# A dilated attention layer laid out by token parity, with values as the stationary operand

## The chip, the cores and the metric

The kernel runs on one core of a Trainium2 chip. The metric is the device time of one execution in microseconds; lower is better. Three runs of the kernel before took 1760.48, 1762.76 and 1765.39 us, so its time is given as the median, 1762.76.

## What is computed

Four transformer layers on 256 tokens of 1024 features, each a mixer and a SwiGLU block with residuals, then one hybrid layer. The mixers are differential attention (layers 0 and 3), latent attention (layer 1) and dilated attention (layer 2); the change is in the last. Its core in the reference:

```
qkv = (h @ w_qkv).reshape(B, S, G, 3, C_HEADS, C_HEAD_DIM)   # G = 3 groups, 16 heads of 64
for g, (window, dilation) in enumerate(((128, 1), (512, 4), (2048, 16))):
    o_g, l_g = _dilated_group(q[:, :, g], k[:, :, g], v[:, :, g], window, dilation)
wts = softmax(stack(lses), axis=0)
o = sum(wts[..., None] * stack(outs), axis=0)
return o.reshape(B, S, C_HEADS * C_HEAD_DIM) @ w_o
```

Here h is the normed input. With 256 tokens, group 0 lets a token attend to tokens at most 64 away; group 1 to all tokens of the same remainder by 4; group 2 to all of the same remainder by 16. Each group has its own softmax and log-sum (`l_g`), and the three outputs are mixed by a softmax over those. All of it is float32.

## The kernel before, in words

Every projection runs in three matmuls per block, since operands are split into a high and a low part of a reduced float32 (`mm3`, lines 184 to 191: high by high, high by low, low by high). `wload` (line 152) fetches a unit of weights (1024 elements in each of 128 partitions), ACT makes its high part (line 158) and DVE its low part (line 159); four raw and six split units can be held. One unit feeds twelve matmuls of 512 columns, six for each of the two tiles of 128 tokens.

The normed input is kept transposed (`hT`, features on partitions, tokens in the columns) and split. `Prep` makes it: `turn` transposes a block of x on PE, DVE multiplies by the gain (L318), ACT writes the high part (L283) and DVE the low part (L284). The factor of each token's norm, `r`, is applied later, where a projection's result is taken out of PSUM. `Prep.half` is called four times, by token tile and half of the features, as the last block of the layer before is added to x.

`layer_c` is the dilated layer. It works group by group in the order (0, first eight heads), (2, both halves), (1, both halves), (0, last eight heads). For groups 1 and 2 the tokens are first put in an order in which those that attend to each other lie side by side: `permuted` copies hT, high part on ACT (L696) and low part on DVE (L698), and the norms go over DRAM by POOL's queue. Within a `step`: queries and keys are projected; their rotation is four DVE operations that end at L384; they are transposed on PE (`to_T`, drained from the list `waiting`); scores come from `qkT` (L735), two heads at a time on the two halves of the rows, 192 keys wide in group 0 and 128 in the others; `heads` adds the mask and takes the maximum on DVE (L537) and the exponential on ACT (L542); `tr4` transposes four blocks of probabilities on PE (L291) into a PSUM bank, which ACT (L524) or DVE (L526) copies out; the values are projected; and the product (L263, by `Chain`, which keeps its matmuls in order) has a 128 x 128 block of probabilities as its stationary operand and 64 columns of values moving. Its output has tokens on partitions. For groups 1 and 2 it goes through DRAM back to the order of tokens, and so do the maxima and sums (`spread`). `dilated` and `total` work out the weights (`merge`) and sum the groups (`wsum`, L860 to L862); the result `on` is transposed on PE and split into `oT` for the output projection (`outacc`), whose first half is issued after both halves of the heads.

PSUM has eight banks: four under the tag acc, two under E, two under T. Tiles of 512 to 1024 elements come from pools of a fixed number of buffers (nine `big` ones of 2048 elements).

The order of the work is set when the program is built: for each engine the framework takes, of the instructions that its own model has as ready, the one that stands earliest in the program, and the engine then runs them in that order. `pump` and `drain` say where in the program the postponed transposes stand. The latent layer (`layer_b`) has a product of another form, which the prediction uses: there the values are stationary and the probabilities move, and heads alternate between the halves of the output partitions.

## Time and profile before

| | us |
|---|---|
| three runs | 1760.48, 1762.76 (median), 1765.39 |
| the profiled execution | 1763.19 |
| its span, first to last instruction | 1761.3 |
| PE busy | 1728.4 |
| DVE busy | 1094.5 |
| ACT busy | 920.0 |
| POOL busy | 75.0 |

The engines are PE (matmuls and transposes; its weight loads are shown as PEld), DVE (element-wise work), ACT (functions and copies), POOL (small work and some transfers) and SP (transfers). A busy time is the union of an engine's instructions. Matmuls overlap each other in the pipeline, so the durations of single ones (some 0.4 us) are longer than the steps between their starts (some 0.23 us); what a matmul costs is read from the steps. Idle time of an engine other than the bounding one costs nothing by itself.

### The profile page before, as it was taken

Reading aid. Unit: us, or ns where it says so; the run is one execution under the profiler, and the core shown is the slowest. Engines: PE = TensorE matmul, PEld = TensorE weight load, DVE = VectorE, ACT = ScalarE, POOL = GpSimd, SP = SyncE. Lnnn points to the kernel's source line nnn. Section 1 sums busy time; section 2 is a strip of 40 time slices with the busy share of each in tenths; the row PEclk is TensorE's granted clock in tenths of the full one; section 3 lists DMA queues with packets and bytes.
Section 4 is the critical chain, followed back from the end, with each engine's and each line's share of the span. In section 5 each row is a group of like instructions: output and inputs, shape, how many; then the busy total and the mean of one; then the engine's idle time right before and its main releaser. Section 6 shows DMA issues by size and latency. Waiting matters only on the chain.

```text
span 1761.3 us, 24095 instructions
## 1 busy us (share of the span) xinstructions
PE 1728.4 (98%) x8944; PEld 1411.0 (80%) x8944; DVE 1094.5 (62%) x1955; ACT 920.0 (52%) x1489; POOL 75.0 (4%) x100
## 2 busy tenths in 40 slices
PE   8999999999999999999999999999999999899998
PEld 6688888877888878788878888877888888688886
DVE  6766545786555575555686744677877567574544
ACT  6655444675444465655655444565544454664443
POOL 1000000101000010000100000000000000010000
PEclk9999999999999999999999999999999999899999
DMA  7346666433666564555545666543567678456662
GB/s 259 112 128 180 185 187 184 148 121 95 187 194 185 177 160 125 163 161 165 159 118 170 187 184 190 176 136 131 167 216 234 190 249 223 144 155 194 190 186 89
DMA packets 168764, 299.53 MB, mean 170 GB/s; under 512 B 20120, under 2 KB 36464, under 8 KB 167880
## 3 DMA queue, kind: packets, MB, share of 16 engines
q1 hardware_dynamic: 164936, 293.52, 54.9%
q0 software_dynamic: 3712, 4.49, 1.0%
q8 instruction: 70, 1.15, 0.3%
q14 instruction: 46, 0.38, 0.1%
HBM read 288.20 MB, written 8.68 MB: 169 GB/s over the span
## 4 chain that ended last, share of the span: by engine, by line
PE 86%; issue 5%; DVE 4%; ACT 2%; DMA 2%; POOL 1%; SPq 0%; POOLq 0%; DVEq 0%; ACTq 0%
PE psacc L191 13%; PE psacc L190 12%; PE psacc L189 12%; PE psE L189 6%; PE psE L191 6%; PE psE L190 6%; PE psT L189 6%; PE psT L190 6%; PE psT L191 6%; PE psT L291 4%; PE psT L263 3%; PE psE L735 2%; PE psE L442 2%; DVE lo L159 1%; PE psE L291 1%
## 5 line engine op out<-in xcount | busy, mean ns | idle before, releaser
L159 DVE TENSOR_TENSOR lo<-raw,hi 128x1024 fp32r<-128x1024 f32 (+1 forms) x528 | 637.3, 1211 | 474.7 <-ACT hi L158 473.2
L158 ACT ACTIVATE hi<-raw 128x1024 fp32r<-128x1024 f32 (+1 forms) x528 | 552.9, 1048 | 588.3 <-PE psacc L191 248.9
L189 PE MATMUL psacc<-hi,big 128*128 128x512 f32 (+1 forms) x1136 | 455.3, 401 | 0.2 <-ACT big L283 0.2
L191 PE MATMUL psacc<-hi,big 128*128 128x512 f32 (+1 forms) x1136 | 449.1, 395 | 0.0
L190 PE MATMUL psacc<-lo,big 128*128 128x512 f32 (+1 forms) x1136 | 447.9, 394 | 0.0
L191 PEld LDWEIGHTS psacc<-hi,big 128*128 128x128 f32 x1136 | 213.8, 188 | 44.9 <-issue 4.2
L190 PEld LDWEIGHTS psacc<-lo,big 128*128 128x128 f32 x1136 | 214.1, 188 | 43.4 <-issue 3.9
L189 PEld LDWEIGHTS psacc<-hi,big 128*128 128x128 f32 x1136 | 214.2, 189 | 40.5 <-issue 1.3
L189 PE MATMUL psE<-hi,big 128*128 128x512 f32 (+2 forms) x568 | 215.3, 379 | 1.0 <-ACT big L283 0.9
L191 PE MATMUL psE<-hi,big 128*128 128x512 f32 (+2 forms) x568 | 213.6, 376 | 0.2 <-DVE big L284 0.2
L190 PE MATMUL psE<-lo,big 128*128 128x512 f32 (+2 forms) x568 | 213.7, 376 | 0.0
L189 PE MATMUL psT<-hi,big 128*128 128x512 f32 (+1 forms) x480 | 178.4, 372 | 0.0
L191 PE MATMUL psT<-hi,big 128*128 128x512 f32 (+1 forms) x480 | 178.3, 372 | 0.0
L190 PE MATMUL psT<-lo,big 128*128 128x512 f32 (+1 forms) x480 | 178.3, 371 | 0.0
L189 PEld LDWEIGHTS psE<-hi,big 128*128 128x128 f32 x568 | 107.6, 189 | 21.0 <-ACT big L283 2.0
L191 PEld LDWEIGHTS psE<-hi,big 128*128 128x128 f32 x568 | 107.5, 189 | 19.0 <-DVE big L284 0.6
L190 PEld LDWEIGHTS psE<-lo,big 128*128 128x128 f32 x568 | 107.5, 189 | 18.4 <-issue 0.4
L189 PEld LDWEIGHTS psT<-hi,big 128*128 128x128 f32 x480 | 90.4, 188 | 15.8 <-issue 0.2
L191 PEld LDWEIGHTS psT<-hi,big 128*128 128x128 f32 x480 | 90.4, 188 | 15.7
L190 PEld LDWEIGHTS psT<-lo,big 128*128 128x128 f32 x480 | 90.4, 188 | 15.6
L542 ACT ACTIVATE p<-psE,st 128x256 f32<-128x256 f32 x96 | 44.5, 472 | 23.5 <-DVE st L540 21.6
L542 ACT ACTIVATE p<-sm,st 128x128 f32<-128x128 f32 (+2 forms) x112 | 45.9, 413 | 19.6 <-DVE st L540 19.6
(288 smaller groups left out, 1557.1 us busy)
## 6 DMA issues: line engine op xcount, KB each, us to landing
raw<-in_f_w_gu SPq DMA_DIRECT2D x176, 512.0 KB, 3.7
raw<-in_f_w_out SPq DMA_DIRECT2D x88, 512.0 KB, 3.6
raw<-in_c_w_qkv SPq DMA_DIRECT2D x72, 512.0 KB, 4.5
raw<-in_a_w_qkv SPq DMA_DIRECT2D x48, 512.0 KB, 3.8
raw<-in_w_gate SPq DMA_DIRECT2D x22, 512.0 KB, 4.2
raw<-in_w_up SPq DMA_DIRECT2D x22, 512.0 KB, 4.2
raw<-in_w_down SPq DMA_DIRECT2D x22, 512.0 KB, 3.5
raw<-in_a_w_o SPq DMA_DIRECT2D x16, 512.0 KB, 3.8
```

Of the source, the lines that this page charges most:

```text
L158: A.activation(hi, raw, AF.Copy)
L159: V.tensor_tensor(lo, raw, hi.bitcast(F32), op=ALU.subtract)
L189: T.matmul(o, a, hi[:, c, :n], start=(first and c == 0), stop=False)
L190: T.matmul(o, a, lo[:, c, :n], start=False, stop=False)
L191: latest[0] = T.matmul(o, b, hi[:, c, :n], start=False, stop=(last and c == nk - 1))
L263: ins = T.matmul(*a, **kw)
L291: return T.transpose(pt[:n, i * 128:(i + 1) * 128], src, ident)
L442: T.matmul(E[e][:, S * a:S * a + S], qT[rows, d0 + a, cs(t)], kT[rows, d0 + a, :], start=True, stop=True)
L542: A.activation(p[:, a], src[:, a], AF.Exp, bias=nmx[:, a:a + 1], scale=scale, accum_out=so[:, a:a + 1])
L735: T.matmul(Es[e][:, k * a:k * a + k], qkT[64 * e:64 * e + 64, d, cs(t)], qkT[64 * e:64 * e + 64, 4 + d, k0:k0 + k], start=True, stop=True)
```

## The change

The 256 tokens are put into two tiles by parity: tile 0 has the even tokens, tile 1 the odd ones. All three groups then use the same layout: the members of groups 1 and 2 lie within one tile and are told apart by masks (same remainder by 2 and by 8 of the place in the tile), and group 0 takes scores over all 256 keys with a band mask by the true positions. `Prep` gets a flag `by2` and writes hT in this order in runs of 64 columns; the norms are brought into it by four small matmuls with columns of the identity (`regroup`). The copies of hT, the transfers through DRAM, `merge` and `wsum` go. The loop is over the halves of the heads; in each, queries, keys and scores of the groups 2, 1, 0 come first, then the weights of the groups are worked out from all maxima and sums, the probabilities are multiplied by them, and the three groups' values are projected. The transposes of the probabilities and the products (`outs`) come later: for the first half of the heads after the next half's first projection, for the second after the first half of the output projection. In `outs` the values are stationary (64 columns), the probabilities move, the groups add up in two PSUM banks, and the result comes out transposed. `Chain.after` keeps a run of products behind the transposes of the next set. The first projection of the layer no longer takes the token tiles one after the other (`tmaj`).

The diff, cut to its core; of `layer_c` the lines that are taken out are not repeated, since the function before stands above.

```diff
-    toks = [n, n // 64 + 4 * (n % 64), n // 16 + 16 * (n % 16)]
+    toks = [n, n // 128 + 2 * (n % 128)]
...
-    put("m1", np.where(p[:, None] // 64 == p[None, :] // 64, 0.0, NEG))
-    put("m2", np.where(p[:, None] // 16 == p[None, :] // 16, 0.0, NEG))
+    put("m1", np.where(p[:, None] % 2 == p[None, :] % 2, 0.0, NEG))
+    put("m2", np.where(p[:, None] % 8 == p[None, :] % 8, 0.0, NEG))
     put("dlt", (p[:, None] % 16 == np.arange(16)[None, :]).astype(np.float32))
-    kb = np.arange(192)[None, None, :] + 64 * np.arange(NT)[None, :, None]
-    put("band", np.where(np.abs(q - kb) <= 64, 0.0, NEG))
+    tk = toks[1].reshape(NT, 128)
+    put("band", np.where(np.abs(tk.T[:, :, None] - toks[1][None, None, :]) <= 64, 0.0, NEG))
...
+            self.last, self.too = None, []
+        def after(self, ins):
+            self.too.append(ins.ins.name)
         def __call__(self, *a, **kw):
             ins = T.matmul(*a, **kw)
+            for name in self.too:
+                tc.add_manual_dep(ins.ins, name, mybir.DependencyInfo(mybir.DependencyClass.NoSync, mybir.DependencyReason.DATA),
+                                  reason="order")
+            self.too = []
...
+    def split_out(dst, blocks, t, pt, scale=None, by2=False):
         n = blocks.stop - blocks.start
         src = pt[:, :n * 128].rearrange("p (c q) -> p c q", c=n)
-        hi, lo = dst[0][:, blocks, cs(t)], dst[1][:, blocks, cs(t)]
+        if by2:
+            src = src.rearrange("p c (e i) -> p c e i", e=2)
+            hi, lo = (z[:, blocks].rearrange("p c (e i) -> p c e i", e=2)[:, :, :, 64 * t:64 * t + 64] for z in dst)
+        else:
+            hi, lo = dst[0][:, blocks, cs(t)], dst[1][:, blocks, cs(t)]
...
+            if self.by2:
+                V.tensor_tensor(v4(xg).rearrange("p c (e i) -> p c e i", e=2), v4(pt).rearrange("p c (i e) -> p c e i", e=2),
+                                gain.unsqueeze(3).to_broadcast([128, 4, 2, 64]), op=ALU.mult)
+            else:
+                V.tensor_tensor(v4(xg), v4(pt), gain.to_broadcast([128, 4, 128]), op=ALU.mult)
+            split_out(self.hT, c, t, xg, by2=self.by2)
...
+        r = small(NT, "rc")
+        def regroup():
+            pt = psum("T")
             for t in range(NT):
+                for e in range(2):
+                    T.matmul(pt[64 * t:64 * t + 64, e:e + 1], ident.rearrange("p (i e) -> p e i", e=2)[:, e], P.r[:, t:t + 1],
+                             start=True, stop=True)
+            V.tensor_copy(r, pt[:, 0:NT])
+        waiting.append(regroup)
+        prs = (((0, 1), (2, 3)), ((0, 1, 2, 3),), ((0, 1, 2, 3),))
+        def qk(g, hb):
             qkT = big([128, 8, S])
+            def consume(a, t, p_):
                 dst = work([128, 512], "qs")
                 A.activation(dst, p_, AF.Copy, scale=r[:, t:t + 1])
                 rope(dst.rearrange("p (h d) -> p h d", d=64)[:, :, 0:16], 8, 8, cos[:, t], sin[:, t], "ra")
                 to_T(qkT, 4 * a, dst, 4, t, (A, V)[a])
             c0 = 3072 * g + 512 * hb
+            proj(hT, [(w, c0, 512), (w, c0 + 1024, 512)], consume)
+            return qkT
+        def numer(g, qkT, p, st):
             drain()
+            k = S if g == 0 else 128
             for t in range(NT):
+                k0 = 128 * t if g else 0
+                for pr in prs[g]:
                     n = len(pr)
                     Es = [psum("E"), psum("E")]
                     for a, d in enumerate(pr):
                         for e in range(2):
+                            rows = slice(64 * e, 64 * e + 64)
+                            T.matmul(Es[e][:, k * a:k * a + k], qkT[rows, d, cs(t)], qkT[rows, 4 + d, k0:k0 + k], start=True, stop=True)
                     for e, E in enumerate(Es):
+                        hs = slice(4 * e + pr[0], 4 * e + pr[0] + n)
+                        heads(E, n, k, 0.125, st[:, t, 0, g, hs], st[:, t, 1, g, hs], p[e][:, t, pr[0]:pr[0] + n], masks[g] if g else band[:, t])
+        def weights(st):
+            mx, sm = st[:, :, 0], st[:, :, 1]
+            nM = small(NT * 8, "nM").rearrange("p (t h) -> p t h", t=NT)
+            V.tensor_tensor(nM, mx[:, :, 0], mx[:, :, 1], op=ALU.min)
+            V.tensor_tensor(nM, nM, mx[:, :, 2], op=ALU.min)
             for t in range(NT):
+                V.tensor_tensor(mx[:, t], nM[:, t].unsqueeze(1).to_broadcast([128, 3, 8]), mx[:, t], op=ALU.subtract)
+                A.activation(mx[:, t], mx[:, t], AF.Exp)
+                V.tensor_tensor(sm[:, t], sm[:, t], mx[:, t], op=ALU.mult)
+                V.tensor_tensor(nM[:, t], sm[:, t, 0], sm[:, t, 1], op=ALU.add)
+                V.tensor_tensor(nM[:, t], nM[:, t], sm[:, t, 2], op=ALU.add)
+                V.reciprocal(nM[:, t], nM[:, t])
+                V.tensor_tensor(mx[:, t], mx[:, t], nM[:, t].unsqueeze(1).to_broadcast([128, 3, 8]), op=ALU.mult)
+        def scaled(g, p, st):
+            k = p[0].shape[3]
+            for t in range(NT):
                 for e in range(2):
+                    for h in range(0, 4, 512 // k):
+                        v = p[e][:, t, h:h + 512 // k]
+                        f = st[:, t, 0, g, 4 * e + h:4 * e + h + 512 // k]
+                        V.tensor_tensor(v, v, f.unsqueeze(2).to_broadcast(v.shape), op=ALU.mult)
+        def vproj(g, hb):
+            vs = work([128, NT, 512], "vs")
+            def consume(a, t, p_):
+                A.activation(vs[:, t], p_, AF.Copy, scale=r[:, t:t + 1])
+            proj(hT, [(w, 3072 * g + 2048 + 512 * hb, 512)], consume)
+            return vs
+        def outs(p, vs, oT):
+            po, pm = [psum("E"), psum("E")], Chain()
+            first = set()
+            def prod(d, cols, g, vc, aT):
+                for e in range(2):
+                    o = po[d // 2][64 * e:64 * e + 64, S * (d % 2) + cols.start:S * (d % 2) + cols.stop]
+                    new = (d // 2, e) not in first
+                    first.add((d // 2, e))
+                    pm(o, vs[g][:, vc, 64 * (2 * d + e):64 * (2 * d + e) + 64], aT[e], start=new, stop=(g == 0 and vc == 1),
+                       skip_group_check=True)
+            def dilated(g):
+                aT = [[tr4([p[g][e][:, t, d] for d in range(4)], (A, V)[e]) for e in range(2)] for t in range(NT)]
+                def prods():
+                    for t in range(NT):
+                        for d in range(4):
+                            prod(d, cs(t), g, t, [aT[t][e][:, d] for e in range(2)])
+                return prods
+            def near(ds):
+                aT = {d: [tr4([p[0][e][:, t, d, cs(c)] for c in range(2) for t in range(NT)], (A, V)[e]) for e in range(2)] for d in ds}
+                def prods():
+                    for d in ds:
+                        for c in range(2):
+                            prod(d, slice(0, S), 0, c, [aT[d][e][:, 2 * c:2 * c + 2].rearrange("p t q -> p (t q)") for e in range(2)])
+                return prods
+            run = None
+            for f in (lambda: dilated(2), lambda: dilated(1), lambda: near((0, 1)), lambda: near((2, 3)), lambda: None):
+                nxt = f()
+                if run:
+                    pm.after(tr4.last)
+                    run()
+                run = nxt
+            for b in range(2):
+                src = po[b].rearrange("p (d e i) -> p d i e", d=2, e=2)
+                hi, lo = (z[:, 2 * b:2 * b + 2].rearrange("p d (i e) -> p d i e", e=2) for z in oT)
+                for d in range(2):
+                    A.activation(hi[:, d], src[:, d], AF.Copy)
+                    V.tensor_tensor(lo[:, d], src[:, d], hi[:, d].bitcast(F32), op=ALU.subtract)
+        oTs = []
+        def late(hb, p, vs):
+            oT = big([128, 2, 4, S], F32R)
+            oTs.append([oT[:, a] for a in range(2)])
+            outs(p, vs, oTs[hb])
+        acc = newacc()
+        todo = None
+        for hb in range(2):
+            p = {}
+            st = small(NT * 48, "stc", bufs=2).rearrange("p (t a g h) -> p t a g h", t=NT, a=2, g=3)
+            for g in (2, 1, 0):
+                qkT = qk(g, hb)
+                if todo is not None:
+                    late(*todo)
+                    todo = None
                 if g:
+                    z = big([128, 2, NT, 4, 128])
+                    p[g] = [z[:, e] for e in range(2)]
                 else:
+                    p[g] = [big([128, NT, 4, S]) for e in range(2)]
+                numer(g, qkT, p[g], st)
+            weights(st)
+            vs = {}
+            for g in (2, 1, 0):
+                scaled(g, p[g], st)
+                vs[g] = vproj(g, hb)
+            todo = hb, p, vs
+        outacc(acc, oTs[0], 0, wo, 0, 4, True, False)
+        late(*todo)
         drain()
         nxt, consume = close()
+        outacc(acc, oTs[1], 0, wo, 4, 4, False, True, consume)
...
-        return lambda: Prep(gains("attn_norm", i))
+        return lambda: Prep(gains("attn_norm", i), i % 3 == 2)
```

## Rows read from the trace of the kernel before

**Rows 1.** The page's first part: busy us (share of the span) and instructions of an engine.
```profile
span 1761.3 us, 24095 instructions
...
PE 1728.4 (98%) x8944; PEld 1411.0 (80%) x8944; DVE 1094.5 (62%) x1955; ACT 920.0 (52%) x1489; POOL 75.0 (4%) x100
```

**Rows 2.** The page's second part: the granted clock in 40 slices, in tenths.
```profile
PEclk9999999999999999999999999999999999899999
```

**Rows 3.** Windows view, the dilated layer: us, engines' busy us, clock, transfers.
```profile
620.10:938.30 318.20, 314.12 (x1666) 253.08 (x1665) 199.04 (x568) 184.35 (x384) 21.15 (x41) 1.00 0.52 149
```

**Rows 4.** Waits view of PE in that stretch: us in total, times, longest.
```profile
PE psT L291 <- DVE qs L384: 3.6, 4, 1.8
```

**Rows 5.** PE's timeline, first projections: start us, us, instruction, count, [idle <- releaser].
```profile
638.27 0.63 PE L291 MATMUL psT<-con,qs 128*128 128x128 f32 x4 [1.84 <-DVE qs L384]
...
641.04 0.39 PE L190 MATMUL psacc<-lo,big 128*128 128x512 f32 x1
...
645.58 0.39 PE L189 MATMUL psacc<-hi,big 128*128 128x512 f32 x1
```

**Rows 6.** Groups by form in that stretch: count, busy us, mean ns, idle before.
```profile
L159 DVE TENSOR_TENSOR lo<-raw,hi 128x1024 fp32r<-128x1024 f32 x81 | 98.7, 1223 | 75.7 <-ACT hi L158 75.4
...
L263 PE MATMUL psT<-vs,aT 128*128 128x64 f32 x256 | 29.4, 273 | 0.0
...
L735 PE MATMUL psE<-big 64*128 64x128 f32 x128 | 18.9, 297 | 0.0
...
L735 PE MATMUL psE<-big 64*128 64x192 f32 x64 | 12.4, 355 | 0.1
L526 DVE COPY aT<-psT 128x512 f32<-128x512 f32 x16 | 11.1, 692 | 9.1 <-PE psT L291 9.0
...
L537 DVE CUSTOM_DVE_ANT_0 sm<-psE,band 128x192 f32<-128x192 f32 x32 | 10.2, 353 | 1.0 <-PE psE L735 0.8
...
L696 ACT ACTIVATE big<-big 128x1024 fp32r<-128x1024 f32 x4 | 8.0, 2036 | 0.0
...
L860 DVE TENSOR_TENSOR ws<-big,f 128x512 f32<-128x512 f32 x8 | 5.5, 681 | 0.0
```

**Rows 7.** PE's timeline, two products of group 0 and their neighbours.
```profile
913.38 3.68 PE L263 MATMUL psT<-vs,aT 128*128 128x64 f32 x32
916.87 0.48 PE L189 MATMUL psacc<-hi,big 128*128 128x512 f32 x1
...
919.49 0.60 PE L291 MATMUL psT<-con,on 128*128 128x128 f32 x4
919.92 3.68 PE L263 MATMUL psT<-vs,aT 128*128 128x64 f32 x32
```

**Rows 8.** PE's timeline: latent layer's product, and four strips in the hybrid layer.
```profile
374.60 2.00 PE L263 MATMUL psT<-big,big 128*64 128x256 f32 x16
376.53 0.64 PE L291 MATMUL psT<-con,qs 128*96 128x128 f32 x4
...
1519.93 1.08 PE L263 MATMUL psacc<-big,ut 128*32 128x128 f32 x32
```

**Rows 9.** Timeline of all engines at the layer's start.
```profile
620.10 0.39 PE L189 MATMUL psE<-hi,big 128*128 128x512 f32 x1
...
620.49 0.62 ACT L283 ACTIVATE big<-xg 128x512 fp32r<-128x512 f32 x1
...
621.14 0.69 DVE L284 TENSOR_TENSOR big<-xg,big 128x512 fp32r<-128x512 f32 x1
...
621.75 0.68 DVE L331 TENSOR_TENSOR x<-psacc,x 128x512 f32<-128x512 f32 x1
```

**Rows 10.** Windows view of two stretches in the hybrid layer.
```profile
1524.50:1529.20 4.70, 3.89 (x35) 3.75 (x34) 3.89 (x9) 1.35 (x3) 2.00 (x2) 1.00 0.14 29
1529.20:1536.00 6.80, 5.75 (x15) 3.38 (x16) 2.02 (x6) 1.92 (x4) 0.63 (x2) 0.50 0.66 158
```

**Rows 11.** PE's timeline between these two.
```profile
1529.56 1.66 PE L291 MATMUL psT<-con,ys 128*128 128x128 f32 x3 [1.17 <-DMA ys<-yo]
```

More of the change, by code (lines that the diff above doesn't have):

```diff
@@ L518, in tr4 @@
         for c, b in enumerate(blocks):
-            transp(pt, c, b)
+            tr4.last = transp(pt, c, b)
         if aT is None:
@@ L669, in layer_c @@
     def layer_c(P, i, j, close):
-        h0, r0 = P.hT, P.r
-        band = work([128, NT, 192], "band")
+        hT = P.hT
+        band = work([128, NT, S], "band")
         o_, w_ = CONST["band"]
@@ L813, in layer_c @@
-        og[0] = work([128, NT, 512], "og0")
-        run(step(0, 0), lambda: permuted(2))
-        og[2] = big([128, NT, D])
-        run(step(2, 0))
-        run(step(2, 1), lambda: permuted(1))
-        spread(2)
-        og[1] = big([128, NT, D])
-        run(step(1, 0))
-        run(step(1, 1))
-        spread(1)
-        oT = pair()
-        st12 = small(NT * 32, "st12", bufs=1)
-        last = step(0, 1)
-        next(last)
-        for hb in range(2):
-            for t in range(NT):
-                dilated(t, hb)
-                if hb == 0:
-                    total(t, 0, og[0][:, t])
```

137 lines of the change are left out of this document (5 added, 132 removed).

## The prediction

> **What bounds the kernel now.** I read the page first: its first part shows PE busy for 1728.4 of 1761.3 us [rows 1], its second a granted clock at nine tenths or more in every slice but one [rows 2]. A busy PE need not be PE at its peak, so the dilated layer was read by itself. It runs from the first matmul of its first projection, at 620.10 us [rows 9], to about 938.3, the same point of the layer after it (that layer's first matmul). In these 318.2 us PE is busy for 314.1, DVE for 199.0 and ACT for 184.4, at a clock of 1.00, which is 2.4 GHz [rows 3]. The waits of that stretch name one that PE had to sit out, for the rotated queries and keys (DVE L384): 3.6 us in four times [rows 4]. So this layer is a chain of PE instructions: what its matmuls cost by their pitch (start to start) is what the layer costs, and a DVE, ACT or POOL instruction taken out gives nothing unless PE waited for it. The steady pitch of a projection's matmul is (645.58 - 641.04) / 20 = 0.227 us [rows 5]. The 80 units of weights of the projections and of the output, twelve matmuls each, stay as they are: 960 x 0.227 = 218 us of the 318. The reader should see in [rows 6] what the rest is made of, for only that can move.
>
> **The change part by part.** The sum is made against the profiled execution: 1763.19 us, span 1761.3, 0.43 above the median 1762.76 of the three runs.
>
> *Values stationary.* Now each product of probabilities and values loads 128 columns of probabilities and streams 64 of values: 256 passes (two for each fp32 product) [rows 6] at (916.87 - 913.38) / 32 = 0.109 us [rows 7], 27.9 us in all, on PE's path. After the change the 64 columns of a head's values are loaded and probabilities are streamed, the heads e = 0 and 1 into the two halves of the output partitions in turn. Groups 1 and 2 have 2 x 2 x 2 x 8 = 64 products of 128 columns (128 passes), group 0 has 2 x 4 x 2 x 2 = 32 of 256 columns (64 passes). The latent layer has just this form: 16 passes of 256 columns into two halves, from 374.60 to 376.53 [rows 8], 0.121 us a pass. So group 0 costs 64 x 0.121 = 7.7 us, and the others, at half the columns, 128 x 0.060 = 7.7: 15.4, a saving of 12.5 us. Bounds: where four strips share the array, 32 passes of 128 columns take 1.08 us [rows 8], 0.034 each; two strips can't be expected to beat that, so the products' lower end is 128 x 0.034 + 64 x 0.068 = 8.7 us. The upper end is no overlap of the halves, each pass at twice its pitch: 30.9 us. I take the latent layer's row, the nearest in shape.
>
> A rule speaks against this step. The Trainium skill (TensorE: Matmul & The Clock Gate, section on packing small matmuls, what overlaps and what doesn't) says that a weight load overlaps a running matmul only where the row groups differ; here both heads use all rows. By it the halves would run one after the other and the 12.5 us would be a loss of 3.0. The trace does not agree: the 16 passes above also use all 128 rows, and transposes, which fill the array with 128 columns each, follow each other at 0.108 us [rows 7], so 256 columns by themselves would be 0.216 and not 0.121.
>
> *Outputs come out transposed.* The 16 transposes of the weighted outputs ("on", four in each of four calls of `total`) go: (919.92 - 919.49) / 4 = 0.108 us each [rows 7], 1.7 us saved.
>
> *Whole band for group 0.* Scores over 256 keys instead of 192: 64 passes. A pass of 192 columns has 355 ns, one of 128 has 297 [rows 6], so 64 more columns are 58 ns; the passes go in pairs of row halves, so 32 x 0.058 = 1.9 us more (3.7 if not in pairs, 0 if they hide in the gaps around them).
>
> *Norms ordered by matmuls.* Four products of one column, eight passes, at most 0.109 each: 0.5 us, between 0.2 and 0.9. They replace the round trip of the norms over DRAM on POOL's queue, which PE never waited for.
>
> *What is off the path.* The permuted copies of hT go (four of 2.04 us on ACT [rows 6] and as many on DVE), as do the weighted sums (DVE L860 to L862, 0.68 each, 24 in all) and the scratch transfers of POOL; in come 32 products of the probabilities by their weights (128 x 512, the shape of L860), some 28 operations on eight columns and a wider mask scan. DVE and ACT stay near their 63% and 58% of [rows 3]. Only the copies can be seen by PE: they stand on ACT ahead of the first projections' evictions, and the longest of PE's four waits (1.84 us before 638.27 [rows 5]) comes while they run. The same waits will be there for the new groups, but short, so I take 2.5 of the 3.6 us off (ends: 0 and 3.6).
>
> *The start of the layer.* Now the first projection works through token tile 0 alone, whose norm is long ready, so PE starts at 620.10 without a wait. With tiles of one parity every matmul needs both halves of the tokens. The block it then wants (tile 1, first half) is written by ACT from 620.49 to 621.11 and by DVE from 621.14 to 621.83 [rows 9]. Two of the first three matmuls can start at 621.11, the third not before 621.83: 1.3 us lost, and a little more if the regrouped reads are slower; I take 1.5 (0 if the build orders ACT otherwise, 2.5 if both engines are a conversion of weights later). Moved to the new split are four ACT and eight DVE operations of 0.6 to 0.7 us, the same in count.
>
> *The end of the layer.* Transposes and products are held back: those of the second half of the heads come in one run after the first half of the output projection. In the first half they have the next projection's matmuls between them. In the second nothing is left: the output's second half waits for them. 64 transposes (7.0 us) go through two PSUM banks, emptied by ACT and DVE in turn (DVE L526, 692 ns [rows 6]). A bank's round is 0.43 of transposes, 0.69 of copy and two hand-overs of about 0.1: 1.3 us, so one set of four each 0.65 instead of 0.43. Sixteen sets lose 3.5 us; the products between the sets cover about 1.2 of it, and a conversion of weights (L159, 1.22) in front of a copy adds 0.7. I take 3.0 lost. Ends: 0, if other work fills the gaps, and 14, if the sets go one after the other (16 x (0.43 + 0.69 + 0.2) - 7.0).
>
> The sum: -12.5 - 1.7 + 1.9 + 0.5 - 2.5 + 1.5 + 3.0 = -9.8 us: 1753.4 against the profiled execution, **1753.0** against the median.
>
> **The rivals.**
> *Fewer waits than I charge.* PE's gaps at the layer's end and start are filled and the early waits go entirely: 3.0 + 1.5 + 1.1 less, 1747.4. For it: PE waited for only 3.6 us in the layer [rows 4]. Against it: nothing independent is left to do before the output's second half.
> *The clock drops in the run at the end.* At a wait of 1.17 us with thin work around it [rows 11] PE was granted 0.50 (1.2 GHz) for 6.8 us, while the stretch before had 1.00 with 3.89 of 4.70 us busy [rows 10]. The new run has transposes with a gap in every set. Half speed for 6.8 us costs 3.4 us (1756.4), for the whole run of some 17 us 8.5 (1761.5). Against it: products lie between the sets, and no gap in it is as long.
> *DVE becomes the bound before the third value projection (the slower side).* Its 16 weighting products per half of the heads stand ahead of the conversions that this projection needs. From the last scores on DVE has 16 mask scans of about 0.5 (353 ns for 192 columns [rows 6] and a read), 16 x 0.68, five conversions of 1.22 (L159), and small operations, rotations and copies that I estimate at 7: 32 us by mean durations, some 27 by starts, since neighbours overlap (the 0.69 from 621.14 is followed 0.61 later [rows 9]). PE has two projections of 48 x 0.227, scores and transposes: 25.5 us, and two or so units converted in advance. It decides once DVE's list outruns PE's by those 2.4 us. Two halves at 4 us give 1761; if all 32 products were exposed, 21.8 us, 1774.8. Against it: DVE's mean share of 63%.
> *The halves don't overlap.* 30.9 instead of 15.4 us of products: 1768.5. Against it: [rows 8].
>
> **How the numbers follow.** Forecast 0.52 (1749 to 1757), fewer waits 0.19, clock 0.15, DVE 0.10, no overlap 0.04. A difference of 0.3% (5.3 us) is about what can be told from none. Below 1757.5 lie the forecast, the fewer waits and a quarter of the clock's case: 0.75. Within 0.3% lie the rest of the clock's, half of DVE's and of the last: 0.18. Slower: 0.07. The range is 1745 to 1762: below it only still denser products, above it most of DVE's case and the last.
>
> **What would show it.** Right: the products as 192 passes near 0.06 and 0.12 us; no "on" transposes; no waits over 1 us for DVE L384's successor; a PE wait of 1 to 2 us at the layer's first matmul on the split of x, and gaps of some 0.2 us between sets of transposes ahead of the last output matmuls; 308 us for the layer. Wrong: passes at 0.12 and 0.24; a clock of 0.50 in the layer; PE waiting for the conversions (DVE L159) in the third value projection; or a time above 1762 or below 1745.

## The result, and the profile after

The changed kernel takes 1745.35 us (four runs, 1745.06 to 1745.89) against 1761.62 us for the kernel before (four runs, 1757.64 to 1765.39). That is 16.3 us less, where 9.8 were forecast. The quotient of these two medians is 0.9908; the ratio on record, an estimate of its own, is 0.9896, with a 95% interval of 0.9879 to 0.9912. The profiled execution took 1745.06 us, 18.1 less than that of before; its page and the view of windows:

```profile
span 1743.3 us, 23729 instructions
...
PE 1710.1 (98%) x8872; PEld 1393.4 (80%) x8872; DVE 1092.7 (63%) x1900; ACT 907.3 (52%) x1467; POOL 55.0 (3%) x61
...
622.33:924.91 302.58, 299.24 (x1609) 238.81 (x1610) 197.03 (x513) 172.47 (x362) 1.10 (x2) 1.00 0.48 142
```

The page has the shape of [rows 1]: PE is busy for 98% of a shorter span. The last line answers to [rows 3]; the clock in the layer is 1.00 as before. A layer is measured here from the last transposes of x ahead of it to the last ones behind it, a mark that both kernels have: 622.59 to 940.78 before, 318.19 us, and 302.58 now, 15.6 less. This mark stands behind the wait at the layer's start, and in the kernel before 11 matmuls of the layer had run ahead of it; counted from the end of the block before (620.10 us before, 620.04 now) it is 320.7 and 304.9 us, 15.8 less. All other layers agree within 0.2 us but the hybrid one, 120.75 before and 118.53 now. Its length moves by itself: in the traces of this study, where its instructions are the same, it has between 116.1 and 124.5 us. So the dilated layer is the change, and the other 2 us are not claimed for it.

The waits of PE in the layer (us in total, times, longest), in answer to [rows 4], and the groups by form, to [rows 6]:

```profile
PE psacc L303 <- DVE x L349: 1.9, 1, 1.9
PE psT L303 <- ACT aT L542: 1.8, 5, 0.8
PE psT L303 <- DVE qs L402: 0.7, 4, 0.2
PE psE L736 <- DVE stc L555: 0.4, 2, 0.2
```

```profile
L303 PE MATMUL psT<-con,big 128*128 128x128 f32 x128 | 18.4, 280 | 1.9 <-ACT aT L542 1.8
L736 PE MATMUL psE<-big 64*128 64x128 f32 x128 | 15.6, 287 | 0.0
...
L736 PE MATMUL psE<-big 64*128 64x256 f32 x64 | 13.1, 402 | 0.4 <-DVE stc L555 0.4
L267 PE MATMUL psE<-aT,vs 128*64 128x128 f32 x128 | 7.9, 276 | 0.0
L267 PE MATMUL psE<-aT,vs 128*64 128x256 f32 x64 | 7.3, 382 | 0.0
```

The reader should see 128 and 64 passes for the products (L267) at 7.9 and 7.3 us of busy time, where one group of [rows 6] had 29.4; scores (L736) that are cheaper for 128 columns although nothing about them was changed; and four waits, of which three are new. PE's timeline (start, us, instruction, count, idle before) shows the two longer ones where the prediction put them, at the layer's start and in the run ahead of the output's second half:

```profile
620.04 0.40 PE L703 MATMUL psT<-r,con 128*64 128x1 f32 x4
622.33 0.66 PE L303 MATMUL psacc<-con,x 128*128 128x128 f32 x4 [1.89 <-DVE x L349]
...
900.72 1.13 PE L303 MATMUL psT<-con,big 128*128 128x128 f32 x8 [0.31 <-ACT aT L542]
901.78 1.97 PE L267 MATMUL psE<-aT,vs 128*64 128x128 f32 x32
903.68 1.09 PE L303 MATMUL psT<-con,big 128*128 128x128 f32 x8
...
906.14 3.67 PE L267 MATMUL psE<-aT,vs 128*64 128x256 f32 x32
```

The products of [rows 7] had 3.49 us for 32 passes; here 32 of 128 columns have 1.90 (901.78 to 903.68), 0.059 each. The wait at the start is for the residual sum in x (DVE L349), not for the split of it that the prediction named, but of the size named.

**Where the 6 us that the sum lacks come from.** Two timelines of PE show it, the first of the kernel before, the second of the changed one: the scores of one group's second token tile, 16 passes each.

```profile
704.73 0.93 PE L735 MATMUL psE<-big 64*128 64x128 f32 x6
705.59 0.33 PE L291 MATMUL psT<-con,p 128*128 128x128 f32 x1
705.85 0.48 PE L735 MATMUL psE<-big 64*128 64x128 f32 x2
706.27 0.33 PE L291 MATMUL psT<-con,p 128*128 128x128 f32 x1
706.35 0.48 PE L189 MATMUL psacc<-hi,big 128*128 128x512 f32 x1
706.67 0.27 PE L291 MATMUL psT<-con,p 128*128 128x128 f32 x1
706.87 0.48 PE L735 MATMUL psE<-big 64*128 64x128 f32 x2
707.28 0.33 PE L291 MATMUL psT<-con,p 128*128 128x128 f32 x1
707.54 0.71 PE L735 MATMUL psE<-big 64*128 64x128 f32 x4
708.18 0.33 PE L291 MATMUL psT<-con,p 128*128 128x128 f32 x1
708.44 0.49 PE L735 MATMUL psE<-big 64*128 64x128 f32 x2
708.85 0.50 PE L190 MATMUL psacc<-lo,big 128*128 128x512 f32 x1
```

```profile
652.24 1.16 PE L736 MATMUL psE<-big 64*128 64x128 f32 x8
653.32 0.50 PE L189 MATMUL psacc<-hi,big 128*128 128x512 f32 x1
653.75 1.16 PE L736 MATMUL psE<-big 64*128 64x128 f32 x8
654.84 0.50 PE L190 MATMUL psacc<-lo,big 128*128 128x512 f32 x1
```

Both stretches hold one projection matmul as well. The first, with five transposes of probabilities among the scores, takes 4.12 us (704.73 to 708.85), the second without them 2.60 (652.24 to 654.84). At 0.11 us for a transpose, 4.12 - 2.60 - 0.55 = 1.0 us is left that no further instruction accounts for: the scores are dear where something stands between them. The change takes all transposes of probabilities out of the scores.

The starts of the single records say where the time goes. In both stretches the first step of a run of scores is 0.213 us and its last 0.202, whether it has two passes or eight, where those between have 0.112; and from a transpose that stands between scores to the next score there are 0.258 us instead of 0.11. A break adds an end, a transpose and a beginning: 0.10 + 0.09 + 0.15 = 0.34 us by this estimate.

### The profile page after: what moved, and what is told of

Its sections match the earlier page's. It is cut to its first block, busy times and chain, and to the rows that moved or that the text cites. A ratio compares the mean times of both kernels' runs of the same rounds, so it can differ in the third digit from the quotient of the medians.

```text
span 1743.3 us, 23729 instructions
## 1 busy us (share of the span) xinstructions
PE 1710.1 (98%) x8872; PEld 1393.4 (80%) x8872; DVE 1092.7 (63%) x1900; ACT 907.3 (52%) x1467; POOL 55.0 (3%) x61
## 4 chain that ended last, share of the span: by engine, by line
PE 87%; issue 5%; DVE 4%; ACT 2%; POOL 1%; DMA 1%; SPq 0%; POOLq 0%; DVEq 0%; ACTq 0%
PE psacc L191 13%; PE psacc L190 13%; PE psacc L189 13%; PE psE L189 6%; PE psE L191 6%; PE psE L190 6%; PE psT L189 6%; PE psT L191 6%; PE psT L190 6%; PE psT L303 4%; DVE lo L159 2%; PE psE L460 2%; PE psE L736 1%; PE psE L303 1%; PE psE L267 1%
## 5 line engine op out<-in xcount | busy, mean ns | idle before, releaser
L189 PE MATMUL psacc<-hi,big 128*128 128x512 f32 (+2 forms) x1152 | 458.6, 398 | 0.2 <-ACT big L295 0.2
L191 PE MATMUL psacc<-hi,big 128*128 128x512 f32 (+2 forms) x1152 | 453.7, 394 | 0.0
L190 PE MATMUL psacc<-lo,big 128*128 128x512 f32 (+2 forms) x1152 | 452.1, 392 | 0.0
L191 PEld LDWEIGHTS psacc<-hi,big 128*128 128x128 f32 x1152 | 216.5, 188 | 45.9 <-issue 4.6
L189 PEld LDWEIGHTS psacc<-hi,big 128*128 128x128 f32 x1152 | 216.7, 188 | 41.5 <-issue 1.7
L189 PE MATMUL psE<-hi,big 128*128 128x512 f32 (+2 forms) x552 | 209.1, 379 | 0.9 <-ACT big L295 0.9
L191 PE MATMUL psE<-hi,big 128*128 128x512 f32 (+2 forms) x552 | 207.2, 375 | 0.2 <-DVE big L296 0.2
L190 PE MATMUL psE<-lo,big 128*128 128x512 f32 (+2 forms) x552 | 207.2, 375 | 0.0
L189 PEld LDWEIGHTS psE<-hi,big 128*128 128x128 f32 x552 | 104.7, 190 | 20.3 <-ACT big L295 2.0
L191 PEld LDWEIGHTS psE<-hi,big 128*128 128x128 f32 x552 | 104.3, 189 | 18.4 <-DVE big L296 0.6
L189 PEld LDWEIGHTS psT<-hi,big 128*128 128x128 f32 x480 | 90.4, 188 | 15.8 <-issue 0.2
L191 PEld LDWEIGHTS psT<-hi,big 128*128 128x128 f32 x480 | 90.4, 188 | 15.7
L190 PEld LDWEIGHTS psT<-lo,big 128*128 128x128 f32 x480 | 90.4, 188 | 15.6
L370 ACT ACTIVATE sg<-psE,r 128x512 f32<-128x512 f32 (+1 forms) x60 | 39.2, 654 | 23.1 <-PE psE L191 22.6
```

The source lines that it names most:

```text
L189: T.matmul(o, a, hi[:, c, :n], start=(first and c == 0), stop=False)
L190: T.matmul(o, a, lo[:, c, :n], start=False, stop=False)
L191: latest[0] = T.matmul(o, b, hi[:, c, :n], start=False, stop=(last and c == nk - 1))
L370: A.activation(sg[t][:, :n], p_, AF.Silu, scale=r[:, t:t + 1])
```

## The experiments

Each ran beside the kernel before on the same chip. As medians of one kernel differ by some 2 us between series, the layer in the trace decides and the ratio on record stands beside it. A wait at the layer's very start lies ahead of the mark and is not in these lengths. In some executions the clock was at 0.50 (1.2 GHz) for 3.4 us in the layer; a projection matmul then has a pitch of 0.43 in place of 0.227, and by these two numbers such a stretch makes the layer 3.4 x (1 - 0.227 / 0.43) = 1.6 us longer, an estimate. "Clock" in the table says where it was so. "Stretch sums" are worked out from the trace: all that PE does between two projection matmuls, from its first start to the start of the second projection matmul behind it, less one pitch of 0.227 and less the waits.

| kernel | median (runs) | ratio to before, 95% | layer, us |
|---|---|---|---|
| before, changed | 1761.62 (4), 1745.35 (4) | 0.9896 [0.9879, 0.9912] | 318.19, 302.59 |
| after_again | 1746.75 (6) | 0.9921 [0.9897, 0.9945] | 302.59 |
| values_alone | 1751.12 (5) | 0.9935 [0.9918, 0.9952] | 305.87 |
| halves_apart | 1753.96 (7) | 0.9951 [0.9935, 0.9966] | 310.01 |
| runs_alone | 1763.78 (11) | 0.9999 [0.9988, 1.0009] | 316.20, clock |
| extra_in_rows | 1759.40 (12) | 0.9988 [0.9977, 0.9999] | 313.40 |
| extra_singly | 1762.32 (11) | 0.9998 [0.9986, 1.0009] | 315.58 |
| scores_whole | 1748.65 (4) | 0.9924 [0.9903, 0.9945] | 306.89, clock |
| scores_broken | 1760.40 (10) | 0.9990 [0.9973, 1.0006] | 313.72 |
| no_hold | 1749.18 (6) | 0.9922 [0.9902, 0.9941] | 306.27, clock |
| late_first | 1748.43 (6) | 0.9913 [0.9888, 0.9938] | 302.68, clock |
| half_first | 1748.35 (5) | 0.9914 [0.9896, 0.9932] | 303.65, clock |
| both | 1746.88 (5) | 0.9911 [0.9892, 0.9929] | 302.80, clock |
| copies_out | 1761.88 (12) | 0.9999 [0.9987, 1.0011] | 318.75, clock |
| filled | 1744.48 (4) | 0.9897 [0.9881, 0.9913] | 298.09 (see there) |

**Values stationary alone (values_alone).** In the kernel before, with the loop over e moved inside, so that the heads take turns:

```diff
-                                pm(po[:, 64 * h:64 * h + 64], aTs[t, e, pr][:, nck * a + c],
-                                   vs[:, t if g else c, 64 * h:64 * h + 64], start=(c == 0), stop=(c == nck - 1))
+                                pm(po[64 * e:64 * e + 64, 128 * d:128 * d + 128], vs[:, t if g else c, 64 * h:64 * h + 64],
+                                   aTs[t, e, pr][:, nck * a + c], start=(c == 0), stop=(c == nck - 1))
```

> The kernel before with one part of the change alone: values stationary, probabilities moving, heads in the two halves of the output partitions; all products 128 columns wide. The output comes out in another layout and is passed on as it is, so what is computed after it is not the reference. My theory (the two halves overlap): the 256 passes of the dilated layer's products fall from 0.109 us to about 0.06 each, 27.9 to 15.4 us, and the time falls by 12 to 13 us, three quarters of what the whole change gave. Rival (the halves don't overlap, and the gain came from elsewhere): passes stay at 0.107 or more and the time stays within 2 us of before. Second rival (the change's gain is long runs): a gain of under 8 us here.

The layer is 12.3 us shorter: the 256 passes have 15.7 us from start to start where they had 27.9. The product step of the sum holds.

**The halves one after the other (halves_apart).** In the changed kernel all products of e = 0 in a run, then all of e = 1.

> The changed kernel, with each run of products ordered by the half of the output partitions (all heads e = 0, then all e = 1) instead of in turn. Theory that the gain is the overlap of the halves: in a run of one half nothing is there to overlap with, passes go from 0.059 and 0.113 us to about 0.107 and 0.214, the products from 14.8 to some 27 us and the time rises by 12 us, to about 1757. Rival (PE's queue looks far enough ahead, or narrow loads alone are the gain): the time stays within 2 us of 1745.4.

The layer is 7.4 us longer, where 12 were expected. A run that has 1.90 and 3.60 us in the changed kernel (32 passes of 128 and of 256 columns) has 3.26 and 4.63 here from start to start. The groups by busy time:

```profile
L267 PE MATMUL psE<-aT,vs 128*64 128x128 f32 x128 | 13.3, 276 | 0.0
L267 PE MATMUL psE<-aT,vs 128*64 128x256 f32 x64 | 9.4, 385 | 0.0
```

The starts of the single records show what overlaps. In the changed kernel passes start in twos, 0.007 us apart, and two take 0.109 us (128 columns) or 0.216 (256). Here the passes inside a half follow each other at 0.109 and 0.216 us each, as expected: two at once take no longer than one. Only around the places where the order goes from one half to the other, from four passes ahead to some four behind, do passes overlap again, which is why the loss is not 12 us. At 0.109 and 0.216 throughout, 128 and 64 passes would have 27.8 us, what the products of the kernel before had (27.9). So the step's gain is the overlap of the two halves of the output, although both use all 128 rows, and by this estimate narrow loads alone give nothing. By the rule of the Trainium skill (TensorE: Matmul & The Clock Gate, the section on packing small matmuls) that the prediction cites, the order of the halves would make no difference; the measurement decides against it here.

**Transposes in runs, in the kernel before (runs_alone).** Those of groups 1 and 2 are held in fours behind the units of the value projection.

```diff
-                        aTs[t, e, pr] = tr4([p_[:, a, cs(c)] for a in range(n) for c in range(nck)], (A, V)[e])
+                        def turn(p_=p_, n=n, e=e, t=t, pr=pr, held=bool(g)):
+                            aTs[t, e, pr] = tr4([p_[:, a, cs(c)] for a in range(n) for c in range(nck)], (A, V)[e], held=held)
+
+                        if g:
+                            waiting.append(turn)
...
```

> The kernel before with another part alone: in groups 1 and 2 the transposes of the probabilities are held back and issued four at a time, each set behind one unit of the value projection's matmuls, in place of one by one as the exponentials end. Nothing is added or left out. New theory (each change of PE between projection, scores and transposes costs some 0.09 us, which my sum left out): about 16 + 40 changes fewer in each direction in the four steps, so 3 to 6 us less, and scores of 128 columns at 0.11 to 0.12 us a pass instead of 0.133. Rival (interruptions are free, the rest of the gain is waits of the first projections): within 1 us of before, or slower since the product now waits for the last copy.

The total does not move, where 3 to 6 us less were expected, and by the total the step would be worth nothing. The trace says otherwise. The stretch sums of scores with the transposes among them fall from 28.46 to 23.74 us (100 score passes in both, 54 and 50 transposes): 4.3 us less for the same work, 0.27 for each of the 16 breaks. This is given back: a wait of 1.72 us for the weights of the groups (DVE L854) at 854.69 is new, waits in all being 0.7 us longer, and behind it the clock falls, by the view of windows:

```profile
856.70:860.10 3.40, 3.40 (x9) 2.65 (x9) 2.98 (x25) 1.10 (x5) 0.80 (x1) 0.51 0.66 173
```

-4.3 + 0.7 + 1.6 = -2.0, which is what the layer shows.

**What a break of the projections costs (extra_in_rows, extra_singly).** My first theory was that each break of the stream of projection matmuls costs 0.09 us: from start to start 992 of their matmuls (960 of the layer, 32 of the block before) went from 240.4 to 235.4 us while the runs of them went from 115 to 58, and the first one behind a break has 0.32 to 0.34 against 0.227. 96 transposes of a constant were added to the value projections of the changed kernel, in six rows or one behind every third matmul.

> The changed kernel with 96 transposes of a constant added, 16 in a row behind each of the six value projections of the dilated layer; their result is not used. By rows of the trace a transpose of 128 columns among others is 0.10 us: 9.6 us, and six more breaks of the stream of projection matmuls. Both theories (a break costs some 0.09 us; a break costs nothing) expect a layer of about 312.5 us, 10 over the changed kernel. It is the base for the next run.

> The same 96 transposes, one behind every third matmul of the value projections: 82 more breaks of the stream of projection matmuls than with rows of 16, and nothing else. Theory, that each change from projection matmuls to something else and back costs 0.09 us or so (the first matmul after one takes 0.32 to 0.34 us against 0.227): 82 x 0.09 = 7.4 us over the run with rows, a layer of 320 us. Rival, that breaks are free and the projections came down for another reason (the copies of hT gone, other traffic): no difference, 312.5. Second rival, that single transposes hide beside the long matmuls: below 312.

PE's timeline with rows, then singly:

```profile
736.33 1.91 PE L306 MATMUL psT<-con 128*128 128x128 f32 x16
738.00 0.48 PE L190 MATMUL psacc<-hi,big 128*128 128x512 f32 x1
```

```profile
744.53 0.27 PE L306 MATMUL psT<-con 128*128 128x128 f32 x1
744.55 0.47 PE L190 MATMUL psacc<-hi,big 128*128 128x512 f32 x1
744.87 0.39 PE L191 MATMUL psacc<-lo,big 128*128 128x512 f32 x1
```

The theory falls. 82 more breaks cost 2.2 us in the layer and not 7.4. The stretch sums give 0.109 us for a transpose in a row and 0.114 for a single one, so 0.4 us of it; the rest lies with four transposes that landed in scores, with waits, and with the matmuls between. The timeline shows why steps from start to start misled: the single transpose has a step of 0.02 and the matmul behind it one of 0.32. Its cost is booked on its neighbour. In the changed kernel the projections' 5.1 us less stand against 3.6 us more for the transposes, and most of both is booking, neither a gain nor a loss.

**What a break of the scores costs (scores_whole, scores_broken).** 32 transposes of a constant in the scores of groups 1 and 2 of the changed kernel, four behind each set, or one behind every second product.

> The changed kernel with 32 transposes of a constant added to the scores of groups 1 and 2, four in a row behind each of the eight sets of eight products; their result is not used. The 96 of the run in rows took 0.11 us each with the way back into the projections: 3.5 us, a layer of 306.1 us. All theories expect that; it is the base for the next run.

> The same 32 transposes, one behind every second product, so that 24 of them stand inside the sets. New theory, since 82 breaks of the projections were found to cost 0.005 us each: what a transpose breaks dearly is a set of scores, whose passes otherwise run in pairs on the two halves of the rows. Taking 16 such breaks out of the kernel before brought its scores and the transposes among them from 28.46 to 23.74 us, four transposes fewer: 0.27 us a break. 24 x 0.18 to 0.27: 4 to 6.5 us over the run with rows, a layer of 310 to 312.6 us, and the scores' 128 passes of 128 columns dearer by most of it. Rival, that the transposes in the kernel before only showed time of their own there: no difference, 306.1.

PE's timelines, whole sets first:

```profile
654.54 1.16 PE L742 MATMUL psE<-big 64*128 64x128 f32 x8
655.63 0.66 PE L303 MATMUL psT<-con 128*128 128x128 f32 x4
```

```profile
654.51 0.49 PE L742 MATMUL psE<-big 64*128 64x128 f32 x2
654.93 0.33 PE L303 MATMUL psT<-con 128*128 128x128 f32 x1
655.19 0.48 PE L742 MATMUL psE<-big 64*128 64x128 f32 x2
```

Two passes and a transpose have 0.68 us (654.51 to 655.19) where two passes of a whole set have 2 x 1.09 / 8 = 0.27 and a transpose 0.11. By the stretch sums the same instructions have 24.23 us broken and 15.98 whole: 8.25 / 24 = 0.34 us a break, more than expected, and what the ends of a run add up to. The layer agrees: 313.72 - 306.89 = 6.8, and 1.6 more for the clock that fell in the run with whole sets. The new theory holds. The trace of before has 23 places where scores follow a transpose of probabilities, 16 of them in groups 1 and 2 and seven in group 0; what the seven cost was not tested.

**The run ahead of the output's second half (no_hold, late_first).** In the changed kernel, without the line that keeps products behind the next set of transposes; and with the run ahead of the output's first half.

```diff
-                    pm.after(tr4.last)
```

> The changed kernel without the order that holds each run of products behind the transposes of the next set. Theory of interruptions: products may now be cut up by transposes, so some tens of changes more and 0 to 3 us slower than 1745.4; the waits of transposes for their copies at the layer's end (1.9 us) may shrink by as much. Rival (waits at the end are what counts): 1.5 to 2 us faster. If the build orders them alike anyway: the same.

```diff
+        late(*todo)
         outacc(acc, oTs[0], 0, wo, 0, 4, True, False)
-        late(*todo)
```

> The changed kernel; the last transposes and products of the dilated layer stand before the first half of the output projection instead of after it, so that its 48 matmuls can fill the gaps between the sets. Theory that the run at the end costs only its gaps (1.9 us of waits and some 0.1 us between sets): 0 to 2 us faster if the fillers come in few pieces. Theory of interruptions: each set that is now cut off by projection matmuls costs 0.09 us, 16 sets 1.5 us, so the two cancel: within 1 us of 1745.4.

Without the hold transposes and products alternate 19 times in place of six: their stretch sums are 3.7 us longer, the waits 1.4 shorter, and 1.6 us of the layer's 3.7 are the clock's. So the hold is worth about 2 us. With the run placed first, its waits for copies fall from 1.9 to 1.1 us and the sums by 0.8, since more of its transposes find projection matmuls to stand among; a drop of the clock hides this in the layer.

**The start (half_first, both, copies_out).** half_first: the block before the layer finishes its last output half by half of the features; both: this with late_first; copies_out: the kernel before without its permuted copies of hT.

```diff
-            for t in range(NT):
-                for n in range(2):
...
+            for t, n in ([(0, 0), (1, 0), (0, 1), (1, 1)] if nmaj else [(0, 0), (0, 1), (1, 0), (1, 1)]):
...
```

> The changed kernel; in the output matmuls of the layer before the dilated one, the first half of the features is finished for both token tiles before the second half is begun, so that what the first projection by parity needs is there earlier. Theory that parity costs PE a wait of 1.9 us at the layer's start: the wait shrinks to under 0.7 and the time falls by 1.2 to 2 us, to about 1743.7. Rival (the wait moves to the second half, whose split now ends as late as before and is followed by less other work): no change within 0.7 us.

> The changed kernel with both orders of work of the two runs before this one. If the two waits are independent, the gains add: up to 3.5 us, about 1742 to 1743.5. If either does nothing by itself: the gain of the other.

> The kernel before without the copies of the normed input into the order of groups 1 and 2 (they take the input in the order of tokens, so the result is not the reference); the scratch transfers stay. My step put the early waits of PE that go with these copies at 2.5 us (the trace of after says 3.1). If the copies are the cause: PE's wait for the rotated queries in the first steps falls from 3.9 us to under 1.2, and the time by 2.5 to 3 us. Rival (the waits come of the first step's order, two projections by token tile): the waits stay and the time is within 1 us of before.

The first two miss: PE now waits 2.3 us at the start, for the norms (POOL L282), because the four norm matmuls stand ahead of everything. Behind it the clock is at 0.50, by the windows of "both":

```profile
622.60:626.00 3.40, 3.40 (x11) 2.77 (x10) 1.98 (x4) 0.73 (x3) 0.55 (x1) 0.50 0.96 319
```

11 instructions of PE ran in these 3.4 us, where the changed kernel had 18 after its wait of 1.89. The third misses too: the time stays, and the waits in the layer fell by 0.9 us only. Without the copies the wait of 1.84 us [rows 5] is gone, its transposes starting at 635.01 without one. But a longer one comes behind it, put down to a conversion of weights on ACT, and that chain of conversions had itself stood idle for a transfer of weights, by the timeline:

```profile
640.31 1.06 ACT L158 ACTIVATE hi<-raw 128x1024 fp32r<-128x1024 f32 x1 [6.13 <-DMA raw<-in_c_w_qkv]
646.68 0.63 PE L291 MATMUL psT<-con,qs 128*128 128x128 f32 x4 [2.42 <-ACT hi L158]
```

Behind this wait the clock fell (0.50 from 647.7 to 651.1). So the copies were not alone in making PE wait in the first projections. The rival on record, the first step's order by token tile, had the time right; it was not run by itself. The windows view from 630 to 637 us shows a third suspect, in the kernel before, in copies_out and in the changed kernel (the last number is GB/s moved):

```profile
630.00:637.00 7.00, 6.44 (x29) 5.00 (x27) 5.09 (x8) 6.58 (x6) 2.00 (x3) 1.00 0.50 28
630.00:637.00 7.00, 7.00 (x34) 5.82 (x33) 4.37 (x7) 3.51 (x4) 1.44 (x3) 1.00 0.50 28
630.00:637.00 7.00, 7.00 (x33) 5.79 (x32) 4.71 (x11) 3.75 (x5) 0.00 (x0) 1.00 0.65 187
```

In the kernel before and its variants values_alone, runs_alone and copies_out, the only traces here in which the norms make their round trip over DRAM, transfers move 28 to 45 GB/s in that stretch; in the changed kernel and all its variants they move 145 to 200. The write of the norms, issued at 627.0 us in the kernel before, takes 7.7 us for 1 KB. That the round trip slows the weights fits all traces, but no run takes it out alone. Which part of the change took these waits away stays open.

**The changed kernel again (after_again) and the start filled (filled).** filled is "both" with the last transposes of x and the norm matmuls held behind the layer's first 12 and 48 projection matmuls.

```diff
-            self.turn(t, h)
+            if self.by2 and t == h == 1:
+                waiting.append(lambda: self.turn(t, h, True))
+            else:
+                self.turn(t, h)
...
-        waiting.append(regroup)
+        put_off(regroup, 2)
```

> The changed kernel once more, unaltered, as a base for the three beside it. In four of the variants of it the clock stood at 0.50 for 3.4 us at the dilated layer's start, behind the same wait of 1.9 us for x that the changed kernel's own trace has without the drop. If the drop belongs to the execution and not to the variants, this run may have it or not: the layer, between the last transposes of x before and after it, 302.6 us without and 304.3 with it, and the ratio to the kernel before 0.988 to 0.992. If the variants' edits brought it, there is no drop here and the ratio is 0.9896 as in the result.

> The changed kernel with three moves: the block before the layer finishes its features half by half, the first half of the output projection stands behind the run of transposes and products, and the last transposes of x and the four norm matmuls stand behind the first 12 and 48 projection matmuls of the layer. The first two moves alone gave a layer of 302.8 us with 2.3 us of waiting at its start and the clock at 0.50 for 3.4 us behind it. Theory, that this wait is there only because nothing ready stands ahead of it: the wait under 0.5 us, no drop, a layer of 299 us, some 3 us below the changed kernel in its median. Rival, that another block of the split input takes its place: a wait of 1 to 2 us before the first or the second unit of weights, 301 to 303 us.

The repeat has the layer of 302.59 us to the hundredth, the same wait of 1.9 us and no drop. Three variants with the same wait (no_hold, late_first, scores_whole) had the drop. Their edits come later in the layer: up to 15 us behind the mark PE's matmuls are the same, in the same order, in all nine traces that have this wait. So a wait of this length can be followed by the drop or not, and most likely that goes with the execution; no kernel was seen both ways.

In filled the wait at the start is gone and the clock stays at 1.00, by its waits in the layer:

```profile
PE psT L302 <- DVE qs L406: 0.9, 5, 0.2
PE psT L302 <- ACT aT L546: 0.6, 1, 0.6
PE psE L740 <- DVE stc L559: 0.4, 2, 0.2
```

As the mark at its start has moved behind 12 matmuls, the block before the layer is counted in: 193.84 + 302.59 = 496.43 us in the changed kernel, 194.11 + 298.09 = 492.20 in filled, 4.2 less. Its median is 2.3 us below that of the changed kernel on the same chip, but the intervals of the two ratios overlap, so the gain is shown by the trace and not by the times alone.

## Why the prediction was wrong, point by point

The direction was right, and so was the mechanism of the largest step. The median of 1745.35 us lies just inside the lower end of the range and 7.7 us below the forecast; by the ratio on record, 0.9896 x 1762.76 = 1744.4 us, just outside. In the layer, from the end of the block before, 15.8 us went against 9.8 forecast; the rows below add up to 15.4 of them:

| step | forecast | measured |
|---|---|---|
| products, and the late run with its waits | -12.5 + 3.0 | -13.1 + 3.9 |
| transposes of "on" | -1.7 | -1.8 |
| scores | +1.9 | -3.6 |
| norms by matmul, transposes of x beside them | +0.5 | +1.0 |
| early waits (L384, now L402) | -2.5 | -3.1 |
| start of the layer | +1.5 | +1.9 |
| a wait of scores for the buffers of the sums (L555), not forecast | 0 | +0.4 |
| pitch of the projections | 0 | about -1.0 |

The products' -13.1 is by starts; the late run is 1.9 of waits for copies and 2.0 of dearer stretches of transposes and products. The scores are by stretch sums, 34.1 us before and 30.5 now, with their transposes taken off at 0.111 us each. The early waits count all idle time ahead of these transposes, 3.95 us before and 0.84 now. Why the pitch fell is not known.

**The step that failed is the one on the scores**, "so 64 more columns are 58 ns; the passes go in pairs of row halves, so 32 x 0.058 = 1.9 us more". For what it speaks of it is near: from start to start a pass of group 0 went from 0.178 to 0.196 us, 1.2 us in 64. What it leaves out is larger and has the other sign: by stretch sums the scores of group 0 rose by 0.5 us only, and those of groups 1 and 2 fell by 4.15. The sum took the scores of groups 1 and 2 as unchanged, and their transposes as moved: it priced these where they went, in the late run, and not where they came from. They had stood inside the sets of scores, where each break costs 0.27 us (runs_alone, 16 of them taken out) to 0.34 (scores_broken); 4.15 us over the same 16 is 0.26. [Rows 6] could not show that, since it gives durations; the timeline of the scores, which the prediction didn't read, does. With -3.6 in place of +1.9 the sum is -15.3 us.

What held: the latent layer's row as the price of the products (0.121 a pass of 256 columns; measured 0.113, and 0.059 for 128); no wait of PE for conversions in the third value projection; no half clock in the run at the end. Of the rivals, "fewer waits" gave nearly the time (1747.4), but by luck: both waits that it had filled are there, 1.9 us each. The rival of halves that don't overlap was priced too high at 30.9 us: passes of one half alone have 0.109 and 0.216 us, 27.8 in all, so it would have cost nothing against the kernel before, and not 3.0. The sentence that the 80 units of projections "stay as they are" holds too; the 5.1 us by starts that seem to contradict it are mostly a matter of booking. Reading the copies of hT as the cause of the early waits was borne out for the first of them only. And that PE "never waited for" the norms' round trip over DRAM is in doubt: PE waited behind weights whose transfers were slow while it ran.

## What to carry over

An instruction that is moved has two prices: one where it goes, and one where it no longer stands between others; read the timeline of both places. Price a kind of matmul by whole stretches, up to the next long matmul, and not by the step to the next start, since a short one's cost can show on its neighbour. Where a small wait sits on the bounding engine, see what it does to the clock behind it before counting it at its length.

## What was not expected of the hardware

A transpose of 128 columns costs 0.109 to 0.114 us wherever it stands among projection matmuls of 512 columns, singly too; among scores with 64 rows and 128 columns it costs 0.27 to 0.34 us more than its own time. Products of 64 columns of weights that alternate between the two halves of the output partitions run two at once: they start 0.007 us apart, and a pass has 0.059 us on the mean where inside one half it has 0.109 (128 columns), 0.113 where it has 0.216 (256). Behind waits of 1.7 to 2.4 us the granted clock went to 0.50 (1.2 GHz) for 3.4 us in seven of the traces; behind the wait of 1.9 us that three of these have at the layer's start it stayed at 1.00 in six others.
